# Down projection by Strassen's seven products instead of eight

## The chip, the cores and the metric

The kernel runs on one core of a Trainium2 chip. The metric is the device time of one execution in microseconds (us). TensorE (PE) multiplies, VectorE (DVE), ScalarE (ACT) and GpSimd (POOL) do elementwise work, and SyncE (SP) issues the DMAs. SBUF is the working memory on the chip, PSUM the eight banks into which PE writes.

## The reference

One layer: an attention sub-layer, then the channel sub-layer, with D = 1024 channels, S = 1024 tokens and D_FF = 2816 (22 blocks of 128 rows):

```python
h = rms_norm(x, ln_ffn_pre[l])
f = (jax.nn.silu(h @ w_ffn_gate[l]) * (h @ w_ffn_up[l])) @ w_ffn_down[l]
x = x + rms_norm(f, ln_ffn_post[l])
```

Everything is float32. The change is in the last product, `(...) @ w_ffn_down`, which is [1024 x 2816] times [2816 x 1024].

## The kernel before

Each float32 operand of a product is split into two parts that TensorE takes, high (h) and low (l): `split_sbuf` (L253) has ACT round the operand into h (L254), and POOL or DVE subtract h from the operand to get l (L256). A product of two operands is then three matmuls, h·h, h·l and l·h, into the same PSUM bank (`mm3`, L267 to L269). Nearly all matmuls here are 128x128 weights times 512 columns.

The channel sub-layer has two stages. **Gate and up** (`ffn_gate_up`, L1205) goes over 11 pairs of row blocks of D_FF. For each pair it makes the gate product, then the up product, each by Strassen's seven half-size products (`product`, L1208, matmuls on L1216) over halves of channels, tokens and the pair's two blocks. The sums of the weights are made beside it (`stationary_parts`, L1162, sums on L1180), up to AHEAD = 6 parts ahead of their use. DVE adds the banks into the four results (L1225), ACT applies silu (L1235), DVE or POOL multiplies gate by up (L1240), and the four tiles of 128x512 go to the scratch tensor `s_aa` in HBM (L1242).

**Down** (`ffn_down`, L1271) reads `s_aa` and `w_ffn_down` back in six portions (2, then five times 4 row blocks), 1024 columns of each at a time, splits them, and runs for each of 8 token tiles and 2 column halves all row blocks of the portion into one bank: 22 x 8 x 2 x 3 = 1056 matmuls. ACT copies the bank into the accumulator `X.acc` for the first portion (L1286), DVE adds it for the others (L1288). During the last portion `finish` (L1295) runs after each token tile: ACT squares its two halves (L1308), DVE makes the reciprocal root's argument (L1313, L245), POOL the power (L247), DVE scales both halves (L1319), POOL adds the residual (L1320), and SP writes them out. The last tile does its work on DVE alone (L1310, L1317).

Memory is handed out by allocators in the kernel (`Mem`, `Zone`, `Block`): the large tile AR holds the split parts, AFm the float32 data. The order of the code isn't the order on the chip: the framework orders each engine's instructions itself, by what is ready first, and each engine then runs its own list strictly in order. [rows 12] shows one case.

Of the kernel before, what the change touches and what calls it, by code (L numbers as in the profile page):

```python
# [11 lines left out]
F32 = mybir.dt.float32  # L12
# [6 lines left out]
P = 128  # L19
# [49 lines left out]
AR_COLS = 38912  # L69
AF_COLS = 13568  # L70
# [5 lines left out]
class Mem:  # L76


    def __init__(self, ap, cols):
        self.ap = ap  # L80
        self.busy = np.zeros(cols // GRAN, dtype=bool)
        self.when = np.zeros(cols // GRAN, dtype=np.int64)
        self.clock = 0

# [36 lines left out]
class Block:  # L121
    def __init__(self, mem, lo, cols):
        self.mem, self.lo, self.cols = mem, lo, cols
        self.ap = mem.ap[:, lo:lo + cols]
# [45 lines left out]
def kernel(  # L170
# [47 lines left out]
    s_aa = scratch("s_aa", (NFF * P, S))  # L218
# [5 lines left out]
    AR = big.tile([P, AR_COLS], F32R, name="AR")  # L224
# [68 lines left out]
    mr, mf, mp = Mem(AR, AR_COLS), Mem(AFm, AF_COLS), Psum(PS)  # L293
# [5 lines left out]
    z_ht, z_w, z_q = Zone(mr, (0, 16384)), Zone(mr, (16384, 24576)), Zone(mr, (24576, 32256))  # L299
    z_c, z_ct = Zone(mr, (32768, 34816)), Zone(mr, (34816, AR_COLS))  # L300
    z_kn = Zone(mr, (32256, 32768))
    z_lat, z_qk, z_v = slots(mr, (2, 7)), slots(mr, (7, 9), (12, 14)), slots(mr, (0, 2), (14, 16))
# [5 lines left out]
    z_wc, z_dn = Zone(mr, (28672, AR_COLS)), Zone(mr, (0, AR_COLS))  # L308
    f_ffn, f_acc, f_dn = Zone(mf, (0, AF_COLS)), Zone(mf, (0, 8192)), Zone(mf, (8192, AF_COLS))
# [530 lines left out]
    def mla_proj(M, n, H):  # L840
        wq = load_hl(w_uq[:, n * 192:n * 192 + P].rearrange("(k p) c -> p k c", p=P), f_raw, z_mw, 384, "p (k c) -> p k c", k=3)
        wk = load_hl(w_ukv[:, n * 256:n * 256 + P].rearrange("(k p) c -> p k c", p=P), f_raw, z_mw, 256, "p (k c) -> p k c", k=2)
        qn, kn = z_qk.alloc(SLOT, SLOT), z_qk.alloc(SLOT, SLOT)
# [361 lines left out]
    def ffn_gate_up(X):  # L1205
        banks = Banks(mp, 0, 8)

        def product(bank, i, first):  # L1208
# [9 lines left out]
            w.free()  # L1218

# [8 lines left out]
        for g in range(NFF // 2):  # L1228
            gate = {}
            for u in range(2):  # L1230
                def done(f, c, src):
# [5 lines left out]
                    else:  # L1237
                        s = gate.pop((f, c))
                        e = nc.vector if isinstance(src, Bank) else nc.gpsimd
                        e.tensor_tensor(out=s.ap, in0=s.ap, in1=src.ap, op=ALU.mult)  # L1240
                        r = (2 * g + f) * P
                        nc.sync.dma_start(s_aa[r:r + P, c * 512:(c + 1) * 512], s.ap)  # L1242
                        s.free()
                    src.free()

                a, b, c = banks.alloc(), banks.alloc(), banks.alloc()
                product(a, MB["11"], True)
                s1 = tmp()
                nc.scalar.copy(s1.ap, a.ap)
                product(b, MB["t2"], True)  # L1250
                u2 = add(s1, b)
                product(c, MB["t1"], True)
                product(b, MB["t3"], False)
# [4 lines left out]
                product(a, MB["21"], False)  # L1258
                done(0, 0, a)
                product(b, MB["t4"], False)  # L1260
# [4 lines left out]
                product(c, MB["22"], False)  # L1265
# [3 lines left out]
                done(0, 1, c12)  # L1269

    def ffn_down(X, f0, n):  # L1271
        aa, ws = [], []
        for f in range(f0, f0 + n):
# [164 lines left out]
```

## Time and profile before

| | |
|---|---|
| median of 3 runs | 2034.36 us (2032.48 to 2034.4) |
| profiled execution | 2036.9 us, of which the profile's span is 2035.0 us |
| granted TensorE clock, mean | 0.992 |
| instructions in the span | 29108 |

A time in the rows counts from the span's start. A line of the profile such as `L256 POOL ... AR<-AFm,AR` names the line of the code, the engine, the tile written and the tiles read.

### The profile page before, as it was taken

The numbers are of one execution on the slowest core, as the hardware profiler recorded it, in microseconds if no ns is written. First come the engines' busy times: TensorE is split into PE (matmuls) and PEld (weight loads), VectorE is DVE, ScalarE is ACT, GpSimd is POOL, SyncE is SP. The second block draws the span as 40 slices with busy tenths as digits, with TensorE's granted clock in tenths as the row PEclk, the third lists the DMA queues.
The fourth block names the chain that finished last, engine by engine and source line by source line (L and its number), as shares of the span: only waits on it lengthen the run. The fifth ranks groups of instructions, "written<-read, shape, count | busy, mean of one in ns | idle before, by whom it ended". The sixth has DMA issues, their size and how long they took to land. (4 is left out here: it accounts for less than half of the span.)

```text
span 2035.0 us, 29108 instructions
## 1 busy us (share of the span) xinstructions
PE 1976.3 (97%) x10656; PEld 1715.3 (84%) x10656; DVE 1156.2 (57%) x2464; ACT 864.2 (42%) x1912; POOL 541.0 (27%) x652
## 2 busy tenths in 40 slices
PE   6999999999999999999999998979999999999998
PEld 6898999999898988988978786757888888888886
DVE  7756757676675667786752354575344444353335
ACT  5445444554544446666653333343333333341102
POOL 2000010200000012222121222356564564462214
PEclk9999999999999999999999999989999999999999
DMA  5212111211212031450043533223222222272204
GB/s 169 69 47 81 44 55 53 57 49 42 77 29 80 29 116 50 130 177 29 32 136 103 176 125 103 85 71 94 73 94 84 71 95 73 95 237 83 83 32 145
DMA packets 148494, 176.52 MB, mean 87 GB/s; under 512 B 13536, under 2 KB 117376, under 8 KB 148352
## 3 DMA queue, kind: packets, MB, share of 16 engines
q1 hardware_dynamic: 148352, 174.68, 27.3%
q8 instruction: 83, 1.36, 0.3%
q14 instruction: 59, 0.48, 0.1%
HBM read 130.54 MB, written 44.11 MB: 86 GB/s over the span
## 5 line engine op out<-in xcount | busy, mean ns | idle before, releaser
L267 PE MATMUL PS<-AR 128*128 128x512 f32 (+3 forms) x2216 | 795.1, 361 | 4.0 <-ACT AR L254 2.5
L269 PE MATMUL PS<-AR 128*128 128x512 f32 (+3 forms) x2216 | 786.3, 356 | 2.6 <-POOL AR L256 2.6
L268 PE MATMUL PS<-AR 128*128 128x512 f32 (+3 forms) x2216 | 784.5, 355 | 3.7 <-POOL AR L256 3.7
L254 ACT CAST AR<-AFm 128x512 fp32r<-128x512 f32 (+4 forms) x514 | 301.7, 610 | 514.1 <-PE PS L1216 207.4
L267 PEld LDWEIGHTS PS<-AR 128*128 128x128 f32 x2216 | 418.1, 189 | 56.8 <-ACT AR L260 3.5
L268 PEld LDWEIGHTS PS<-AR 128*128 128x128 f32 x2216 | 419.0, 189 | 47.8 <-POOL AR L256 4.5
L269 PEld LDWEIGHTS PS<-AR 128*128 128x128 f32 x2216 | 417.9, 189 | 46.3 <-POOL AR L256 3.5
L256 POOL TENSOR_TENSOR AR<-AFm,AR 128x512 fp32r<-128x512 f32 (+4 forms) x203 | 309.2, 1529 | 461.7 <-ACT AR L254 397.4
L1216 PE MATMUL PS<-AR 128*128 128x512 f32 x1848 | 425.7, 392 | 6.1 <-POOL AR L256 4.9
L1216 PEld LDWEIGHTS PS<-AR 128*128 128x128 f32 x1848 | 349.3, 189 | 82.2 <-POOL AR L256 6.2
L256 DVE TENSOR_TENSOR AR<-AFm,AR 128x512 fp32r<-128x512 f32 (+5 forms) x311 | 213.1, 714 | 109.3 <-ACT AR L254 81.8
L260 ACT CAST AR<-PS 128x512 fp32r<-128x512 f32 (+3 forms) x320 | 134.5, 440 | 149.5 <-DVE AFm L388 75.4
L1225 DVE TENSOR_TENSOR AFm<-AFm,PS 128x512 f32<-128x512 f32 x110 | 75.2, 684 | 180.3 <-PE PS L1216 179.6
L261 DVE TENSOR_TENSOR AR<-PS,AR 128x512 fp32r<-128x512 f32 (+3 forms) x320 | 152.9, 496 | 38.0 <-ACT AR L260 36.5
L619 POOL CAST AR<-AR 128x128 fp32r<-128x128 f32 (+1 forms) x128 | 43.1, 337 | 456.0 <-PE PS L690 262.4
L649 ACT ACTIVATE AFm<-PS,nm 128x1024 f32<-128x1024 f32 (+3 forms) x192 | 142.5, 745 | 45.9 <-DVE nm L648 28.8
L648 DVE TENSOR_REDUCE nm<-PS 128x1 f32<-128x1024 f32 (+3 forms) x192 | 143.5, 751 | 3.2
L1288 DVE TENSOR_TENSOR AFm<-AFm,PS 128x512 f32<-128x512 f32 x80 | 54.4, 685 | 103.1 <-PE PS L269 103.1
L1180 DVE TENSOR_TENSOR AFm<-AFm 128x512 f32<-128x512 f32 x66 | 70.4, 1066 | 68.4 <-DMA s_aa<-AFm 29.7
L627 POOL MEMSET AR<- 128x256 f32 x64 | 22.3, 349 | 295.3 <-PE PS L269 200.3
L707 PE MATMUL PS<-AR 128*128 128x256 f32 x640 | 94.9, 290 | 0.1
L609 PE MATMUL PS<-idf,AFm 128*128 128x128 f32 x576 | 88.6, 275 | 2.2 <-ACT AFm L741 0.9
(133 smaller groups left out, 1551.9 us busy)
## 6 DMA issues: line engine op xcount, KB each, us to landing
AFm<-in_w_in_dram SPq DMA_DIRECT2D x72, 192.0 KB
AFm<-in_w_ffn_gate_dram SPq DMA_DIRECT2D x22, 512.0 KB
AFm<-in_w_ffn_up_dram SPq DMA_DIRECT2D x22, 512.0 KB
s_aa<-AFm SPq DMA_DIRECT2D x44, 256.0 KB
AFm<-in_w_ffn_down_dram SPq DMA_DIRECT2D x22, 512.0 KB
AFm<-s_aa SPq DMA_DIRECT2D x22, 512.0 KB
AFm<-in_x_dram SPq DMA_DIRECT2D x16, 512.0 KB
AFm<-in_w_in_dram SPq DMA_DIRECT2D x32, 256.0 KB
```

The lines of the kernel that those rows point to most:

```text
L254: nc.scalar.copy(h, src)
L256: e.tensor_tensor(out=l, in0=src, in1=f32v(h), op=ALU.subtract)
L260: nc.scalar.copy(h, src)
L261: nc.vector.tensor_tensor(out=l, in0=src, in1=f32v(h), op=ALU.subtract)
L267: nc.tensor.matmul(o, lhsT=sh, rhs=mh, start=first, stop=False)
L268: nc.tensor.matmul(o, lhsT=sh, rhs=ml, start=False, stop=False)
L269: nc.tensor.matmul(o, lhsT=sl, rhs=mh, start=False, stop=last)
L609: nc.tensor.transpose(tb.ap[:, q * P:(q + 1) * P], C[:, (g + q) * P:(g + q + 1) * P], idf)
L648: nc.vector.tensor_reduce(out=nm[:, m:m + 1], in_=src, axis=ax, op=ALU.max, negate=True)
L649: nc.scalar.activation(out=dst, in_=src, func=ACTF.Exp, bias=nm[:, m:m + 1], scale=1.0, accum_out=ss[:, m:m + 1])
L707: nc.tensor.matmul(sb.ap[:, p * 256:(p + 1) * 256], lhsT=qs.ap[:, m * 256 + v * P:m * 256 + v * P + P], rhs=slots[p]["kT"][:, m, :], start ...
L1216: nc.tensor.matmul(o, lhsT=v[:, ws, k], rhs=m, start=first and k == 0 and x == 0, stop=k == 3 and x == 2, skip_group_check=True)
```

## The change

The down product is done by Strassen's seven products (the form with fifteen additions) too, over halves of tokens (512), of output columns (512) and the two row blocks of a pair. Per pair there are 7 x 4 token tiles x 3 = 84 matmuls, for 11 pairs 924.

- *Token sums in the gate and up stage.* After the up product of a pair, three sums on DVE and one on POOL are made of the four tiles, and seven tiles, not four, go to HBM (`s_a7`).
- *Weight sums.* `down_parts` makes eight differences of 128x512 on DVE for each group of two pairs (the last group has one pair), and splits what the seven products need: 28 parts for a group, 14 of tokens and 14 of weights, every fourth one with its subtraction on DVE, the others on POOL. With one pair there are 14 token parts of 256 columns and 7 weight parts of 512.
- *Products.* Each of the five full groups and the short one runs two token halves (hf), in each the products m1, m6, m5, m7, m2, m4, m3 for two token tiles (tl). m7 and m4 accumulate further into m6's bank, m2 into m1's, m3 into m5's; each product's bank is added to the accumulators by DVE (in the first group copied by ACT, except for m7 and m3). So m7 waits until m6's bank has been read. In the last group POOL adds m1 to three accumulators for each of 4 token tiles, and `finish` runs after m4 and m3; in its second half the order is all products of one token tile, then of the other.
- *Prefetch.* `fill_down` issues further units while four blocks of 1024 columns are free in AR; the first ones during the last seven products of the gate and up stage.
- *Memory.* AR is two tiles now; the second one's place is taken over by the accumulators after the gate and up stage. Two zones of the attention stage (`z_qk`, `z_v`) lie elsewhere.

```diff
+                if u == 1:
+                    x11, x12, x21, x22 = gate[0, 0], gate[1, 0], gate[0, 1], gate[1, 1]
+                    q1 = pair(x21, x22, ALU.add, nc.vector)
+                    q2 = pair(q1, x11, ALU.subtract, nc.vector)
+                    q3 = pair(x11, x21, ALU.subtract, nc.gpsimd)
+                    q4 = pair(x12, q2, ALU.subtract, nc.vector)
+                    for i, t in zip(ORDER, (x11, q2, q1, q3, x12, x22, q4)):
+                        keep(i, t)
...
+    GROUPS = [(g, min(2, NFF // 2 - g)) for g in range(0, NFF // 2, 2)]
+    ORDER = ("m1", "m6", "m5", "m7", "m2", "m4", "m3")
...
+        def part(src):
+            b = z_dn.alloc(1024, 1024)
+            n = src.shape[1]
+            h, l = b.ap[:, 0:n], b.ap[:, n:2 * n]
+            turns[0] += 1
+            split_sbuf(src, h, l, "dve" if turns[0] % 4 == 0 else "pool")
+            return b, h, l
...
+            elif i == "m6":
+                t1 = [diff(v[0, 1], v[0, 0]) for v in B]
+                t2 = [diff(v[1, 1], t.ap) for v, t in zip(B, t1)]
+                ops = [t.ap for t in t2]
...
+    def ffn_down(X):
+        where = {"m1": "a", "m6": "b", "m5": "c", "m7": "b", "m2": "a", "m4": "b", "m3": "c"}
+        for g, kt in GROUPS:
+            first, last = g == 0, g + kt == NFF // 2
+            for hf in range(2):
+                todo = [(i, tl) for i in ORDER for tl in range(2)]
+                if last and hf == 1:
+                    todo = [(i, tl) for tl in range(2) for i in ORDER]
+                for i, tl in todo:
...
+                    for k in range(kt):
+                        _, bh, bl = bs[i][k]
+                        for x, (st_, mv) in enumerate(((sh, bh), (sh, bl), (sl_, bh))):
+                            nc.tensor.matmul(pb.ap, lhsT=st_[:, k, ts_], rhs=mv,
...
+                    for o in to:
+                        if first and i in ("m1", "m6", "m5", "m2", "m4"):
+                            nc.scalar.copy(o, pb.ap)
+                        else:
+                            nc.vector.tensor_tensor(out=o, in0=o, in1=pb.ap, op=ALU.add)
+                    if last and i == "m1":
+                        for o in (acc[t][:, 1], acc[t + 4][:, 1], acc[t + 4][:, 0]):
+                            nc.gpsimd.tensor_tensor(out=o, in0=o, in1=m1, op=ALU.add)
...
+                    if last and i == "m4":
+                        finish(X, t + 4)
+                    if last and i == "m3":
+                        finish(X, t)
...
+    def fill_down():
+        while mr.room(0, AR_CUT) >= 4096:
+            u = next(down, None)
```

## Rows read from the trace of the kernel before

**Rows 1.** The page's first part: busy us, share of the span, instructions.

```profile
PE 1976.3 (97%) x10656; PEld 1715.3 (84%) x10656; DVE 1156.2 (57%) x2464; ACT 864.2 (42%) x1912; POOL 541.0 (27%) x652
```

**Rows 2.** Stretches: busy us (instructions) of PE, PEld, DVE, ACT, POOL; clock, DMA, GB/s.

```profile
1500.00:1600.00 100.00, 99.68 (x440) 82.19 (x439) 40.99 (x55) 31.31 (x52) 55.69 (x41) 1.00 0.27 85
...
1786.00:1900.00 114.00, 114.00 (x504) 94.39 (x503) 50.16 (x49) 35.00 (x44) 40.66 (x17) 1.00 0.42 139
1900.00:2025.00 125.00, 125.00 (x553) 103.49 (x553) 49.55 (x79) 18.14 (x36) 35.55 (x25) 1.00 0.26 89
2025.00:2035.00 10.00, 0.78 (x4) 0.32 (x2) 4.33 (x8) 1.45 (x4) 2.33 (x3) 0.66 0.28 105
```

**Rows 3.** Timeline of PE: the down stage's first and last matmul.

```profile
1786.26 0.39 PE L267 MATMUL PS<-AR 128*128 128x512 f32 x1
...
2025.39 0.39 PE L269 MATMUL PS<-AR 128*128 128x512 f32 x1
```

**Rows 4.** Groups by line: busy us, mean ns, idle us before and what ended it.

```profile
L1216 PE MATMUL PS<-AR 128*128 128x512 f32 x1848 | 425.7, 392 | 6.1 <-POOL AR L256 4.9 <-ACT AFm L1249 0.7 <-DVE AFm L1225 0.3
...
L1288 DVE TENSOR_TENSOR AFm<-AFm,PS 128x512 f32<-128x512 f32 x80 | 54.4, 685 | 103.1 <-PE PS L269 103.1
```

**Rows 5.** Timeline of DVE in the last two finishes: start, us, what.

```profile
2020.38 0.69 DVE L1288 TENSOR_TENSOR AFm<-AFm,PS 128x512 f32<-128x512 f32 x1 [0.81 <-PE PS L269]
2021.92 0.16 DVE L1313 TENSOR_TENSOR ss<-ssh 128x1 f32<-128x1 f32 x1 [0.85 <-ACT AFm L1308]
...
2022.99 1.41 DVE L1319 SCALAR_TENSOR_TENSOR AFm<-AFm,rs_r 128x512 f32<-128x512 f32 x2 [0.73 <-POOL rs_r L247]
...
2027.25 0.67 DVE L1288 TENSOR_TENSOR AFm<-AFm,PS 128x512 f32<-128x512 f32 x1
...
2030.45 1.42 DVE L1317 SCALAR_TENSOR_TENSOR AFm<-AFm,rs_r 128x512 f32<-128x512 f32 x2 [0.73 <-POOL rs_r L247]
```

**Rows 6.** Timeline of POOL in the same finish.

```profile
2022.41 0.55 POOL L247 TENSOR_TENSOR rs_r<-rs_v,mhalf 128x1 f32<-128x1 f32 x1 [1.03 <-DVE rs_v L245]
2023.87 2.91 POOL L1320 TENSOR_TENSOR AFm<-AFm 128x512 f32<-128x512 f32 x2 [0.92 <-issue]
```

**Rows 7.** Timeline of ACT in the same finish.

```profile
2021.16 0.63 ACT L1308 ACTIVATE AFm<-AFm 128x512 f32<-128x512 f32 x1 [0.70 <-DVE AFm L1288]
```

**Rows 8.** Timeline of DVE inside the gate and up stage.

```profile
1590.77 2.64 DVE L1180 TENSOR_TENSOR AFm<-AFm 128x512 f32<-128x512 f32 x2 [0.98 <-issue]
...
1607.55 0.69 DVE L256 TENSOR_TENSOR AR<-AFm,AR 128x512 fp32r<-128x512 f32 x1
1608.15 0.68 DVE L1225 TENSOR_TENSOR AFm<-AFm,PS 128x512 f32<-128x512 f32 x1
```

**Rows 9.** Timeline of POOL at the same place.

```profile
1589.87 1.29 POOL L1240 TENSOR_TENSOR AFm<-AFm 128x512 f32<-128x512 f32 x1 [2.87 <-DVE AFm L1225]
1591.14 1.72 POOL L256 TENSOR_TENSOR AR<-AFm,AR 128x512 fp32r<-128x512 f32 x1
```

**Rows 10.** Single lines: duration in ns, min/median/max.

```profile
L1288 DVE TENSOR_TENSOR AFm<-AFm,PS x80: 673/686/689, 1819.9 to 2027.3; 128x512 f32<-128x512 f32 x80
...
L1180 DVE TENSOR_TENSOR AFm<-AFm x63: 681/842/1753, 1356.2 to 1753.0; 128x512 f32<-128x512 f32 x63
...
L256 POOL TENSOR_TENSOR AR<-AFm,AR x18: 2388/2410/3399, 1790.0 to 1942.2; 128x1024 fp32r<-128x1024 f32 x18
```

**Rows 11.** Groups by line and shape, from 1300 us on.

```profile
L254 ACT CAST AR<-AFm 128x512 fp32r<-128x512 f32 x173 | 106.5, 621 | 253.1 <-PE PS L1216 207.4 <-issue 29.1 <-DMA AFm<-in_w_ffn_up_dram 3.7
...
L1180 DVE TENSOR_TENSOR AFm<-AFm 128x512 f32<-128x512 f32 x64 | 69.0, 1078 | 56.0 <-DMA s_aa<-AFm 29.7 <-DMA AFm<-in_w_ffn_up_dram 11.5 <-issue 8.6
```

**Rows 12.** Timeline of ACT at the end of the gate and up stage.

```profile
1765.33 1.05 ACT L254 CAST AR<-AFm 128x1024 fp32r<-128x1024 f32 x1 [2.75 <-DMA AFm<-s_aa]
...
1770.14 0.59 ACT L1249 COPY AFm<-PS 128x512 f32<-128x512 f32 x1 [1.36 <-PE PS L1216]
```

**Rows 13.** Who waited for whom in SP's queue, gate and up stage.

```profile
SPq L1168 <- POOL AR L256: 167.8, 37, 8.1
```

More of the change, by code (lines that the diff above doesn't have):

```diff
@@ L69 @@
 AR_COLS = 38912
+AR_CUT = 30720
 AF_COLS = 13568
@@ L76, with __init__ @@
 class Mem:
-    def __init__(self, ap, cols):
-        self.ap = ap
+    def __init__(self, *aps):
+        self.aps, cols = [], 0
+        for ap in aps:
+            self.aps.append((cols, ap))
+            cols += ap.shape[1]
         self.busy = np.zeros(cols // GRAN, dtype=bool)
@@ L83, in __init__, with view, room @@
         self.clock = 0
+    def view(self, lo, cols):
+        at, ap = [x for x in self.aps if x[0] <= lo][-1]
+        assert lo + cols - at <= ap.shape[1]
+        return ap[:, lo - at:lo - at + cols]
+    def room(self, lo, hi):
+        return GRAN * int((~self.busy[lo // GRAN:hi // GRAN]).sum())
     def release(self, lo, cols):
@@ L1206, in ffn_gate_up, with product @@
         banks = Banks(mp, 0, 8)
-        def product(bank, i, first):
+        def product(bank, i, first, end):
             X.fill()
@@ L1218, in product @@
             w.free()
+            if end:
+                for q in range(4):
+                    mr.release(7168 * q + 1024 * i, 1024)
+                X.fill_down()
         def tmp():
@@ L1230, in ffn_gate_up @@
             for u in range(2):
+                end = u == 1 and g == NFF // 2 - 1
                 def done(f, c, src):
@@ L1257, in ffn_gate_up @@
                 done(1, 1, c22)
-                product(a, MB["21"], False)
+                product(a, MB["21"], False, end)
                 done(0, 0, a)
-                product(b, MB["t4"], False)
+                product(b, MB["t4"], False, end)
                 c21 = add(s1, b)
@@ L1264, in ffn_gate_up @@
                 done(1, 0, c21)
-                product(c, MB["22"], False)
+                product(c, MB["22"], False, end)
                 c12 = add(u2, c)
@@ L1269, in ffn_gate_up @@
                 done(0, 1, c12)
[L1271 to L1293 removed]
+                if u == 1:
[6 more added lines that the diff above has]
+                        keep(i, t)
+                        t.free()
+                    x21.free()
@@ L1395, in fill @@
             X.parts.append(b)
-    X.fill = fill
+    X.down, down, X.wl = [], down_parts(), None
+    def fill_down():
+        while mr.room(0, AR_CUT) >= 4096:
+            u = next(down, None)
+            if u is None:
+                return
+            X.down.append(u)
+    X.fill, X.fill_down = fill, fill_down
     mix_out(X, prefetch)
-    h2 = mr.ap[:, 0:28672]
-    X.h2v = h2.rearrange("p (q i h c) -> p q i h c", q=4, i=7, h=2)
+    X.h2v = AR[:, 0:28672].rearrange("p (q i h c) -> p q i h c", q=4, i=7, h=2)
     ffn_gate_up(X)
-    for b in X.h2:
-        b.free()
-    X.dn = Banks(mp, 0, 8)
+    X.m1 = [f_m1.alloc(512, 512) for _ in range(4)]
+    AFb = turn.tile([P, AR_COLS - AR_CUT], F32, tag="turn", name="AFb")
+    f_acc = Zone(Mem(AFb), (0, 8192))
     X.acc = [f_acc.alloc(D, 1024) for _ in range(NT)]
-    down = [ffn_down(X, 0, 2)] + [ffn_down(X, f0, 4) for f0 in range(2, NFF, 4)]
-    next(down[0])
-    for i, d in enumerate(down):
-        if i + 1 < len(down):
-            next(down[i + 1])
-        next(d, None)
+    ffn_down(X)
 _INS = ['x', 'positions', 'ln_mix_pre', 'w_in', 'lambda_q1', 'lambda_k1', 'lambda_q2', 'lambda_k2', 'da_subln',
```

151 lines of the change are left out of this document (112 added, 39 removed).

## The prediction

> **What bounds the kernel now.** I read the engines' shares first: PE is busy 97% of the span, DVE 57%, ACT 42%, POOL 27% [rows 1]. A busy share of PE is not yet a bound, so the stages come next: in the gate and up stage and through the down stage PE has no gap at full clock (100 of 100 us, 114 of 114, 125 of 125), while DVE and POOL have room, POOL 56 of 100 us in the first and 41 of 114 in the second [rows 2]. The idle times agree: PE lost 6.1 us in all before the 1848 gate and up matmuls, and in the down stage it is DVE that waited for PE, 103.1 us [rows 4]. So the down stage costs what its matmuls cost. From its first matmul to its last plus one step (1786.26 to 2025.6) there are 1056 in 239.3 us, 0.2267 us each [rows 3]. From there to the end of the span lie 9.4 us of the last tile's norm.
>
> **The matmuls.** 1056 become 924 of the same shape: 132 x 0.2267 = **29.9 us** less, as long as PE stays without gaps. A full group then takes 168 x 0.2267 = 38.1 us, the five of them 190.4 us, the last group 19.0 us. The rest of the sum is what the other engines make of that.
>
> **What DVE and POOL share.** An instruction of DVE with two operands in SBUF and one of POOL don't run at the same time here. POOL's product from 1589.87 ends at 1591.16; the first of two DVE sums, issued at 1590.77, falls in it; POOL's next takes 1.72 in place of 1.29, and DVE's second sum ends 0.55 after that, so two sums of 0.6 took 2.64 [rows 8, 9]. One DVE instruction thus held POOL up by 0.43 us. Sums on SBUF run from 681 to 1753 ns, while evictions, with one operand in PSUM, stay within 673 to 689 [rows 10].
> The Trainium skill (SBUF — State Buffer, Who interferes with whom) has the same as a lock: a DVE instruction with two SBUF inputs contends with a POOL instruction that reads SBUF, and the loser "fully blocks"; with one SBUF input it doesn't. By that rule the forecast below stands; if the two merely overlapped, the sum would be the 2021 of the first rival. The rows here bear the rule out.
>
> **A full group of the down stage** (38.1 us of PE):
> - POOL: 21 of 28 subtractions x 1.29 [rows 9] = 27.1 us. DVE: 7 subtractions and 8 differences, each 0.60 from start to start [rows 8] = 9.0 us, holding POOL up 15 x 0.43 = 6.5. POOL with that: 33.6 us of 38.1.
> - DVE besides: 28 evictions x 0.69 [rows 10] = 19.3 us, so 28.3 without waits. ACT: 28 x 0.62 [rows 11] = 17.4 us.
> - DVE's waits for POOL: at worst each of the 15 waits out a whole POOL instruction, 19.4 us, DVE 47.7, and the group is 9.6 us longer than PE's 38.1: +48 us for five. At best, none of it reaches PE: 0 (less than nothing is excluded, as matmuls without gaps can't be closer). The nearest row: the sums of the gate and up stage took 1.08 on the mean against 0.68 alone, a wait of 0.40 [rows 10, 11] with POOL busy 0.56 [rows 2]; at POOL's 0.71 that is 0.5, DVE 36 us of 38.1.
> At 95%, in strict order, DVE isn't a bound but a queue. What stands in it behind a sum that waits is evictions, and PE waits for those: m7 can't start in m6's bank until it is read, and between m6's end and m7's start for a tile lie 3 x 6 matmuls = 4.1 us. Four differences in a row, each alternating with a POOL instruction, take 4 x 1.7 = 6.8. So I expect PE to lose something in each group and take a quarter of the way to the worst case: **+12 us** (0 to 48).
>
> **The last group** is where most is given back. Before, the part of the span that answers to it is 84 matmuls plus the 9.4 us: 28.4 us, for the finishes were spread over 44 us of matmuls, one each 5.44 us. Now all eight finishes, 28 evictions and 12 extra POOL sums stand against 19.0 us of matmuls.
> - POOL: 12 + 14 sums x 1.29 = 33.5, eight powers x 0.55 [rows 6] = 4.4, held up by 16 DVE instructions x 0.43 = 6.9: 44.8 us. It starts 1.8 us in (m1's 3 matmuls, its eviction), and after the last power come 4.6 us, from the last scaling at 2030.45 to the end of the span [rows 5]. Floor: 51.2 us.
> - Ceiling, if DVE keeps each finish whole before it takes the next eviction: from an eviction's end (2021.07) to the end of the scaling (2024.40) 3.33 us [rows 5], by a square more (0.73, [rows 7] and its read-out) after m4, where both halves wait: 4 x 4.75 + 3 x 4.02 with their evictions, 7.75 for the last (2027.25 to the end), 20 other evictions = 13.8, the start 0.9, and some 10.5 in which evictions of m6 wait for POOL's sums (four ahead of m6's second tile, a finish's two sums and one more in each pass of the second half): 64 us.
> The order isn't that of the code: the framework put a cast of the down stage ahead of a copy of the stage before it [rows 12]. So I go nearer the floor's side, without reaching it, since the list is fixed beforehand: 57 us, **+28.6** against 28.4 (22.8 to 35.6). If PE falls to its lower clock in the gaps (0.66 in the last row of [rows 2], after it stopped), the m7 and m4 that evictions wait for add up to 5.4 us (24 matmuls x 0.227) within that ceiling.
>
> **Gate and up.** Per pair DVE gets three sums, POOL one, some 11 x (3 x 0.60 + 1.29) = 34 us in all if it all fell on PE. It is covered: DVE is busy 41 of 100 us there and POOL 56 [rows 2], weight parts are six products ahead (6 x 2.72 us), and the next eviction that PE needs has a whole product of 2.72 us. Seven writes and not four per pair add 33 x 256 KB, 21 GB/s beside 85; SP's queue, where the next weight load stands behind the writes, already waits 167.8 us for POOL to free buffers, at most 8.1 at a time [rows 13], inside the 16 us of lead. 0, up to 34. In the down stage 31.7 MB in some 200 us are 158 GB/s, where 139 took 0.42 of the DMA engines [rows 2]: 0. Memory moves and the accumulators' new place, free once the last gate and up matmul has run: 0, as the first eviction into it comes two products later; a few us either way in the attention stage, where I see no wait that they add.
>
> **The sum.** 2035.0 − 29.9 + 12 + 28.6 = 2045.7 of span; the profiled execution lies 1.9 above its span, and 2.5 above the median of the runs, so **2045 us**.
>
> **Rivals.**
> 1. *Faster: the queues never reach PE.* DVE's waits stay under the 4.1 us of slack in every group, and the last group packs down to its floor: 2035 − 29.9 + 22.8 = 2028, 2027 as a median; without any exclusion between DVE and POOL 6.9 less, some 2021. It decides on whether m6's evictions come within 4.1 us. For it: POOL and DVE each have 5 to 12% spare in a group, and units are prepared 9 or more ahead. Were the last group's work hidden altogether, 2005; its POOL work alone (38 us) speaks against that.
> 2. *No change:* 2 us lost in the groups and 28.6 in the last one: 2035.
> 3. *Slower by more: DVE's queue is the bound.* 24 to 48 us in the groups: 2057 to 2081. For it: bursts of four differences; against: the mean wait of 0.40.
> 4. *Slower, in the gate and up stage:* the sums hold up evictions there, by up to 34: up to 2079. Against: the cover above.
> That the change doesn't cut the matmuls to 924 can't be, by its loops.
>
> **Chances.** My forecast, 2039 to 2057, 0.40; rival 1, 0.26; rival 2, 0.16; rival 3, 0.13; rival 4, 0.05. A measurement tells 0.2% (4 us) from no change. Faster 0.26, the same 0.16, slower 0.58. The range runs from 2020, the first rival's packed case, to 2070, inside the third.
>
> **What would show it.** Right: in the trace after, 924 matmuls on the down stage's line, gaps of PE of a few hundred ns to some us ended by DVE evictions in each full group, longest after m6; from the last group's first matmul to the end 51 to 64 us with POOL busy throughout and PE mostly idle. Wrong: full groups without gaps (then the 12 is nothing), a last group much under 51 us (then POOL's sums overlap more than I think), or PE waiting in the gate and up stage by more than its 6 us of now.

## The result, and the profile after

The changed kernel takes **2116.18 us** (median of 4, 2114.78 to 2122.17) beside 2034.38 us for the kernel before (4 runs): a ratio of **1.0413**, interval 1.0396 to 1.0430. The forecast was slower, 2045, and the range ended at 2070, so both the amount and the range were wrong. (The ratio is an estimate of its own and not the quotient of the two medians, 1.0402, which lies in the interval.) The profiled execution's span is 2113.8 us, 78.8 more than before.

The first row answers to [rows 1], the second fence to [rows 2] (columns as there).

```profile
PE 1985.2 (94%) x10524; PEld 1700.1 (80%) x10524; DVE 1315.3 (62%) x2627; ACT 905.0 (43%) x2033; POOL 700.7 (33%) x774
```

```profile
1500.00:1600.00 100.00, 94.17 (x404) 75.19 (x403) 51.63 (x60) 31.65 (x55) 56.75 (x39) 1.00 0.26 85
...
1936.30:1940.00 3.70, 0.40 (x2) 0.03 (x1) 3.70 (x6) 0.62 (x1) 3.48 (x3) 0.89 0.42 135
1940.00:1945.00 5.00, 5.00 (x12) 3.94 (x13) 3.54 (x6) 0.00 (x0) 0.00 (x0) 0.50 0.28 95
1945.00:1980.00 35.00, 35.00 (x154) 28.93 (x153) 25.20 (x32) 15.39 (x27) 27.14 (x19) 0.99 0.41 136
...
2055.50:2113.80 58.30, 24.94 (x86) 16.99 (x84) 41.45 (x63) 10.48 (x32) 41.30 (x34) 0.70 0.27 99
```

PE is busy only 9 us more, with 132 matmuls fewer; DVE has 159 us more and POOL 160. In the gate and up stage, where PE had 100 of 100 us, it now has 94 (first window), though no other engine but its weight loads is busy for more than 57 of 100. Next the timeline of PE (start, us, operation, count, and in brackets the idle time before it and what ended it); it answers to [rows 3].

```profile
1505.94 8.66 PE L1230 MATMUL PS<-AR,ARb 128*128 128x512 f32 x36 [1.97 <-DVE AFm L1243]
...
1541.64 3.06 PE L1230 MATMUL PS<-AR,ARb 128*128 128x512 f32 x12 [1.97 <-DVE AFm L1243]
...
1824.91 5.86 PE L1230 MATMUL PS<-AR,ARb 128*128 128x512 f32 x24 [3.51 <-DVE AFm L1243]
1830.61 8.34 PE L1417 MATMUL PS<-AR 128*128 128x512 f32 x36
1843.61 7.34 PE L1417 MATMUL PS<-AR 128*128 128x512 f32 x24 [4.66 <-ACT AFb L1425]
1857.01 34.63 PE L1417 MATMUL PS<-AR 128*128 128x512 f32 x144 [6.06 <-DVE AFb L1427]
1895.41 41.28 PE L1417 MATMUL PS<-AR 128*128 128x512 f32 x168 [3.78 <-DVE AFb L1427]
1940.00 41.15 PE L1417 MATMUL PS<-AR 128*128 128x512 f32 x168 [3.31 <-DVE AFb L1427]
1984.45 76.08 PE L1417 MATMUL PS<-AR 128*128 128x512 f32 x321 [3.30 <-DVE AFb L1427]
```

L1230 is the gate and up matmul, L1417 the down matmul, L1243 and L1427 the evictions by DVE. From such rows each span divides at the first matmul of either stage and the first of the last group (the 841st of the down line, its start counted back from the end of its block at 0.2267 us each):

| us | before | after | difference | forecast |
|---|---|---|---|---|
| start of gate and up | 1347.7 | 1350.3 | +2.7 | 0 |
| gate and up | 438.6 | 480.3 | **+41.7** | **0** |
| five full groups (190.4 of matmuls) | | 225.0 | **+34.6** | **+12** |
| last group | 28.4 | 58.2 | +29.8 | +28.6 |
| 132 matmuls fewer | | | −29.9 | −29.9 |
| sum | | | +78.9 | +10.7 |

The stage that I had priced at nothing cost most. The +2.7 at the start says nothing: in the runs below, none of which changes the attention stage's instructions, the gate and up stage starts between 1345.5 and 1350.1. The groups by line (from 1300 us on; columns as in [rows 4]) show who waited:

```profile
L1230 PE MATMUL PS<-AR,ARb 128*128 128x512 f32 x1464 | 354.5, 401 | 27.8 <-DVE AFm L1243 21.4 <-POOL ARb L270 2.4 <-ACT ARb L268 1.6
...
L1417 PE MATMUL PS<-AR 128*128 128x512 f32 x924 | 228.7, 410 | 41.2 <-DVE AFb L1427 25.0 <-DVE rs_v L259 7.1 <-ACT AFb L1425 4.7
...
L1326 DVE TENSOR_TENSOR AFm<-AFm 128x512 f32<-128x512 f32 x44 | 53.6, 1231 | 20.9 <-POOL AR L270 13.9 <-DMA AFm<-in_w_ffn_down_dram 7.0
...
L1268 DVE TENSOR_TENSOR AFm<-AFm 128x512 f32<-128x512 f32 x33 | 38.6, 1171 | 26.4 <-POOL AFm L1260 25.7
```

PE waits for DVE's evictions in both stages. The two kinds of sums that the change adds, L1268 (token sums) and L1326 (weight differences), take 1171 and 1231 ns where one alone takes 681 [rows 10]. What this does to PE is seen in DVE's own timeline, here at one gap of each stage:

```profile
1533.40 0.69 DVE L1268 TENSOR_TENSOR AFm<-AFm 128x512 f32<-128x512 f32 x1 [1.41 <-POOL AFm L1260]
1534.01 1.78 DVE L1194 TENSOR_TENSOR AFm<-AFm 128x512 f32<-128x512 f32 x1
1535.72 0.68 DVE L1268 TENSOR_TENSOR AFm<-AFm 128x512 f32<-128x512 f32 x1
1536.32 0.68 DVE L1194 TENSOR_TENSOR AFm<-AFm 128x512 f32<-128x512 f32 x1
1536.92 1.78 DVE L1268 TENSOR_TENSOR AFm<-AFm 128x512 f32<-128x512 f32 x1
1538.62 0.68 DVE L270 TENSOR_TENSOR ARb<-AFm,ARb 128x512 fp32r<-128x512 f32 x1
1539.23 1.76 DVE L1194 TENSOR_TENSOR AFm<-AFm 128x512 f32<-128x512 f32 x1
1540.91 0.68 DVE L1243 TENSOR_TENSOR AFm<-AFm,PS 128x512 f32<-128x512 f32 x1
...
1932.40 2.88 DVE L1326 TENSOR_TENSOR AFm<-AFm 128x512 f32<-128x512 f32 x2
1935.20 0.68 DVE L1427 TENSOR_TENSOR AFb<-AFb,PS 128x512 f32<-128x512 f32 x1
1935.80 1.18 DVE L270 TENSOR_TENSOR AR<-AFm,AR 128x512 fp32r<-128x512 f32 x1
1936.90 0.68 DVE L1427 TENSOR_TENSOR AFm<-AFm,PS 128x512 f32<-128x512 f32 x1
1937.50 1.16 DVE L1326 TENSOR_TENSOR AFm<-AFm 128x512 f32<-128x512 f32 x1
1938.58 0.67 DVE L1427 TENSOR_TENSOR AFm<-AFm,PS 128x512 f32<-128x512 f32 x1
1939.18 1.27 DVE L1427 TENSOR_TENSOR AFb<-AFb,PS 128x512 f32<-128x512 f32 x2
```

From 1533.40 to 1540.91 DVE works without a pause on seven instructions with two operands in SBUF, and only then on the eviction that the matmuls of 1541.64 wait for. At 1541.64 PE has been idle for 1.97 us. The engine is half empty over 100 us and full over the 8 us that count. In the down stage sums and evictions alternate, and the two-operand instructions (L1326 and L270 here) take 1.16 us and more where one alone takes 0.68; the first eviction of the row at 1939.18 is the one that the matmuls of 1940.00 wait for.

The Trainium skill (SBUF — State Buffer, Who interferes with whom) names what sets the two kinds apart: a DVE instruction with at most one SBUF input, outside DVE's two-port modes, doesn't contend with GpSimd. The trace agrees: all 110 evictions L1243 took 673 to 690 ns, the sums among them up to 1.78 us.

### The profile page after: what moved, and what is told of

It is laid out like the page before. It is cut to its first block, busy times and chain, and to the rows that moved or that the text cites. A ratio compares the mean times of both kernels' runs of the same rounds, so it can differ in the third digit from the quotient of the medians.

```text
span 2113.8 us, 29579 instructions
## 1 busy us (share of the span) xinstructions
PE 1985.2 (94%) x10524; PEld 1700.1 (80%) x10524; DVE 1315.3 (62%) x2627; ACT 905.0 (43%) x2033; POOL 700.7 (33%) x774
## 3 DMA queue, kind: packets, MB, share of 16 engines
q1 hardware_dynamic: 170992, 191.98, 28.6%
## 5 line engine op out<-in xcount | busy, mean ns | idle before, releaser
L281 PE MATMUL PS<-AR 128*128 128x512 f32 (+3 forms) x1368 | 501.6, 368 | 3.5 <-ACT AR L268 2.9
L283 PE MATMUL PS<-AR 128*128 128x512 f32 (+3 forms) x1368 | 494.8, 362 | 2.1 <-POOL AR L270 2.1
L282 PE MATMUL PS<-AR 128*128 128x512 f32 (+3 forms) x1368 | 492.3, 360 | 3.8 <-POOL AR L270 3.8
L270 POOL TENSOR_TENSOR AR<-AFm,AR 128x512 fp32r<-128x512 f32 (+3 forms) x206 | 300.4, 1479 | 273.0 <-ACT AR L268 228.9
L1230 PE MATMUL PS<-AR,ARb 128*128 128x512 f32 x1464 | 354.5, 401 | 27.8 <-DVE AFm L1243 21.4
L268 ACT CAST AR<-AFm 128x512 fp32r<-128x512 f32 (+5 forms) x461 | 248.2, 574 | 290.0 <-PE PS L1417 98.6
L1230 PEld LDWEIGHTS PS<-AR,ARb 128*128 128x128 f32 x1464 | 277.6, 191 | 102.0 <-DVE AFm L1243 27.1
L281 PEld LDWEIGHTS PS<-AR 128*128 128x128 f32 x1368 | 258.5, 189 | 30.0 <-ACT AR L268 3.4
L282 PEld LDWEIGHTS PS<-AR 128*128 128x128 f32 x1368 | 259.0, 189 | 27.4 <-POOL AR L270 4.2
L283 PEld LDWEIGHTS PS<-AR 128*128 128x128 f32 x1368 | 258.3, 189 | 26.3 <-POOL AR L270 3.0
L1417 PE MATMUL PS<-AR 128*128 128x512 f32 x924 | 228.7, 410 | 41.2 <-DVE AFb L1427 25.0
L1417 PEld LDWEIGHTS PS<-AR 128*128 128x128 f32 x924 | 182.9, 200 | 86.8 <-DVE AFb L1427 22.9
L270 DVE TENSOR_TENSOR AR<-AFm,AR 128x512 fp32r<-128x512 f32 (+4 forms) x255 | 169.5, 698 | 77.3 <-ACT AR L268 50.0
L270 POOL TENSOR_TENSOR ARb<-AFm,ARb 128x512 fp32r<-128x512 f32 (+2 forms) x96 | 133.9, 1406 | 136.4 <-ACT ARb L268 131.9
L1243 DVE TENSOR_TENSOR AFm<-AFm,PS 128x512 f32<-128x512 f32 x110 | 75.0, 683 | 150.4 <-PE PS L1230 148.5
L281 PE MATMUL PS<-ARb,AR 128*128 128x256 f32 (+2 forms) x470 | 153.3, 328 | 1.1 <-DVE ARb L275 0.5
L282 PE MATMUL PS<-ARb,AR 128*128 128x256 f32 (+2 forms) x470 | 151.0, 321 | 0.0
L283 PE MATMUL PS<-ARb,AR 128*128 128x256 f32 (+2 forms) x470 | 150.2, 320 | 0.0
```

Of the source, the lines that this page charges most:

```text
L268: nc.scalar.copy(h, src)
L270: e.tensor_tensor(out=l, in0=src, in1=f32v(h), op=ALU.subtract)
L281: nc.tensor.matmul(o, lhsT=sh, rhs=mh, start=first, stop=False)
L282: nc.tensor.matmul(o, lhsT=sh, rhs=ml, start=False, stop=False)
L283: nc.tensor.matmul(o, lhsT=sl, rhs=mh, start=False, stop=last)
L1230: nc.tensor.matmul(o, lhsT=v[:, ws, k], rhs=m, start=first and k == 0 and x == 0, stop=k == 3 and x == 2, skip_group_check=True)
```

## The experiments

Theory A throughout: instructions of DVE and POOL with both operands in SBUF stand in each other's way, and evictions stand behind them in DVE's list. The rivals differ by place. Stage times come from profiled executions; that of the gate and up stage differs by some 9 us between kernels that leave it unchanged (480.3, 481.6, 486.9 and 489.4 in the four that change the down stage alone), so smaller differences there say nothing. The five groups of runs that leave the groups alone differ too (215.0 to 225.7), more by what the lower clock costs after the gaps (4.9 to 13.5 us) than by the gaps (18.4 to 23.3 us).

### The address of the second part of AR

In the trace, matmuls with weights in ARb took 394 ns (median), those in AR 389, and from start to start 0.2333 us against 0.2267. With 1464 of them that is 9.8 us of PE's time. The first run moves ARb by 32 bytes, from byte 196128 to 196160; the second puts it behind AR at byte 140416.

```diff
-    ARb = turn.tile([P, AR_COLS - AR_CUT], F32R, tag="turn", name="ARb")
+    ARb = turn.tile([P, AR_COLS - AR_CUT + 8], F32R, tag="turn", name="ARb")[:, 8:]
...
```

> The changed kernel with its second part of AR (and the accumulators that take its place) moved by 32 bytes, so that it begins on a multiple of 64 bytes in a partition; nothing else. In the trace after, the gate and up matmuls whose weights lie in the second part take 394 ns (median) where those with weights in the first take 389, and one follows the other in 0.233 us in place of 0.227. Theory A, the address: all go back to 389 ns, the stage of 480 us (1350.3 to 1830.6) is 8 to 10 us shorter, span about 2105. Rival, the split into two tiles as such (waits on two tiles): 394 stays, no change, 2114.

Measured: 2112.30 us, ratio 1.0397 (1.0382 to 1.0413); matmuls 392 ns, the stage 482.0. Alignment is a part of it at most.

```diff
-    AFm = big.tile([P, AF_COLS], F32, name="AFm")
+    rest = ctx.enter_context(tc.tile_pool(name="rest", bufs=1))
+    AFm = rest.tile([P, AF_COLS], F32, name="AFm")
...
```

> The changed kernel with the second part of AR right behind the first in SBUF (at byte 140416 of a partition; it lay at 196128, or 196160 in the run that only aligned it), where the same weights lay before the change, and the float32 tile behind it. Matmuls with weights there took 394 ns, 392 when aligned to 64 bytes, 389 before the change. Theory, the address: 389 ns, the gate and up stage 7 to 10 us shorter than 480, span about 2105. Rival, the two tiles (each matmul waits on and signals for both): 392 to 394 stays, no change.

Measured: 2109.60 us, ratio 1.0377 (1.0361 to 1.0392); 389 ns, but the stage still 480.8. The matmuls got faster, and PE waited longer (30.6 us of gaps from 1384 us on, 26.6 before the edit): with the sums in place, the side engines set the pace. The whole span is 4.1 us shorter (2109.7), but that lies ahead of the stage, which starts at 1345.8 here. Whether the 9.8 us count without the sums is asked of the run with all additions left out, below, which changes other things too.

### The token sums, and what about them costs

```diff
-                    q1 = pair(x21, x22, ALU.add, nc.vector)
...
-                    for i, t in zip(ORDER, (x11, q2, q1, q3, x12, x22, q4)):
+                    for i, t in zip(ORDER, (x11, x12, x21, x22, x12, x22, x11)):
...
```

> The changed kernel without the three DVE sums and the POOL sum of a pair; seven tiles are still written, some of them twice the same, so the result of the down product is left out of account. The stage of gate and up is 41.6 us longer after the change (480.3 against 438.6), 27.8 us of it in gaps of PE that mostly end with an eviction on DVE. Theory A, the sums on DVE (the first waits for POOL's product, each may wait out a POOL instruction, and evictions stand behind them): the gaps fall to about the 6 us of before, the stage to about 455 (the address effect of some 9 us stays, and the end of the stage, where the down parts begin, some 5), span about 2089. Rival B, the seven writes, which hold up the weight loads in SP's queue: stage stays within 5 us of 480.

Measured: 2085.22 us, ratio 1.0259 (1.0244 to 1.0275), the stage 452.1. The four sums of each pair, with the buffers that they hold, cost 28 us. The three additional writes don't:

```diff
-                    for i, t in zip(ORDER, (x11, q2, q1, q3, x12, x22, q4)):
+                    for i, t in zip(ORDER, (x11, q2, q1, q3)):
...
```

> The changed kernel with all four sums made, but only four of the seven tiles written (the others read back in their place, so the down product's input is partly replaced). Theory A, the sums on DVE: the gate and up stage stays within 5 us of 480. Rival B, the writes in SP's queue: the stage falls by 20 to 30 us, as the loads of weights come earlier. The two together, should both be needed: 5 to 15 us.

Measured: 2112.96 us, ratio 1.0399 (1.0381 to 1.0416), the stage 483.2.

If DVE's list is the trouble, should the sums go to POOL?

```diff
-                    q1 = pair(x21, x22, ALU.add, nc.vector)
+                    q1 = pair(x21, x22, ALU.add, nc.gpsimd)
...
```

> The changed kernel with all four token sums of a pair on POOL. Theory A (without the sums the gate and up stage took 452 us in place of 480, so DVE's sums and what stands behind them cost some 28 us): DVE no longer waits for POOL's product, POOL gets 3 x 1.29 = 3.9 us more for each pair of 38, its instructions hold up DVE's weight sums a little more; the stage falls to 452 to 462 us, span 2088 to 2098. Rival, the exclusion alone counts, whoever makes the sums: the stage stays over 470.

Measured: 2143.44 us, ratio 1.0547 (1.0531 to 1.0562), the stage 513.6: A's number missed, and on the wrong side; the rival's "over 470" holds, but it doesn't say why the stage gets 33 us longer. The timelines of POOL and of DVE at one pair's end show why:

```profile
1540.61 6.39 POOL L1268 TENSOR_TENSOR AFm<-AFm 128x512 f32<-128x512 f32 x4
1546.96 2.49 POOL L1194 TENSOR_TENSOR AFm<-AFm 128x512 f32<-128x512 f32 x2
```

```profile
1548.25 1.74 DVE L1194 TENSOR_TENSOR AFm<-AFm 128x512 f32<-128x512 f32 x1 [3.77 <-POOL AFm L1194]
1549.92 0.67 DVE L1243 TENSOR_TENSOR AFm<-AFm,PS 128x512 f32<-128x512 f32 x1
```

The four sums stand ahead of POOL's weight sums, DVE waits 3.77 us for the first of these, and the eviction stands behind. So it isn't one engine's time but both lists, and what crosses between them.

Three runs ask whether it is the work of the sums or the buffers that they hold (four of 512 columns in the zone from which the raw weights, 2048 columns each, are loaded too).

```diff
-                    q1 = pair(x21, x22, ALU.add, nc.vector)
...
+                    for q, z in ((q1, x21), (q2, x11), (q3, x22), (q4, x12)):
+                        nc.scalar.copy(q.ap, z.ap)
```

> Leaves out the four token sums of each pair: four ACT copies of the tiles fill the same buffers, and the same seven writes follow. Theory A (the sums' own time on DVE and POOL, and the lock between them, hold up the evictions): the gate and up stage 450 to 460 us, as without sums (452), median 2084 to 2092. Rival (what costs is that the four extra buffers and the eviction of gate into them come later, or ACT's queue): the stage stays at 475 to 483, median 2107 to 2113.

Measured: 2103.28 us, ratio 1.0348 (1.0329 to 1.0368), the stage 473.9: A missed, and the time lies next to the rival's. Without any sum on DVE or POOL, 22 of the 28 us remain.

```diff
...
+                    for q, z in zip(qs, (x21, x11, x22, x12)):
+                        nc.scalar.copy(q.ap[:, 0:8], z.ap[:, 0:8])
...
+                        nc.sync.dma_start(s_a7[g, n + 3][:, 0:8], t.ap[:, 0:8])
...
```

> Leaves out the four token sums of each pair; four buffers of 512 columns are taken at the same place all the same, ACT copies 8 columns into each (four short instructions), three tiles are written whole and the four buffers' 8 columns, and then they are given back. Theory A (memory: the raw weights' buffers of the next pairs come free later, the weight sums that need them bunch up on DVE, and evictions queue behind): the gate and up stage 468 to 480 us, median 2100 to 2112, as with the full copies (473.6). Rival (the work: what ACT's full copies cost was ACT's time): 450 to 457, as without sums (452), median 2082 to 2090.

Measured: 2095.26 us, ratio 1.0319 (1.0303 to 1.0334), the stage 469.9: the buffers alone, with next to no work, keep 18 of the 28 us of the stage. The median is only 10 us above that of the run without sums, below A's forecast, for the five groups took 215.0 here and 225.1 there: after three of its five gaps the clock stayed full. The opposite, the work without the buffers:

```diff
-    z_wc, z_dn = Zone(mr, (28672, AR_CUT), (AR_CUT, AR_COLS)), Zone(mr, (0, AR_CUT))
+    z_wc, z_qs, z_dn = Zone(mr, (AR_CUT, AR_COLS)), Zone(mr, (28672, AR_CUT)), Zone(mr, (0, AR_CUT))
...
-                    t = tmp()
+                    t = z_qs.try_alloc(512) or tmp()
```

> The four token sums are written to 2048 columns of AR (taken from the zone of the split weight parts, which keeps 8192 columns for 8 parts in place of 10) and not to the zone of the raw weights. They come out rounded to the matmul's type, so the result is less exact. Theory A (memory): the stage 455 to 468 us where it is 480, median 2090 to 2104. Rival (the work of the sums on DVE and POOL): 478 to 490, median 2112 to 2124; so too if the two parts fewer now hold up the splits.

Measured: 2097.73 us, ratio 1.0327 (1.0310 to 1.0345), the stage 474.8, between the two forecasts, the median inside A's. All weights lie in ARb here, the 384 others too, which is 2.6 us of it at 0.0067 each.

What the buffers do is seen in SP's queue (who waited for whom: us, times, longest; gate and up stage), from the kernel after, the one without sums, the one that holds buffers, and the one with room, in this order; it answers to [rows 13]:

```profile
SPq L1182 <- POOL ARb L270: 170.1, 15, 15.3
```

```profile
SPq L1182 <- POOL ARb L270: 138.3, 23, 8.2
```

```profile
SPq L1182 <- POOL ARb L270: 198.2, 15, 16.0
```

```profile
SPq L1182 <- POOL ARb L270: 156.2, 38, 8.0
```

The load of a raw weight waits for buffers that POOL's subtractions free. Before, no wait was above 8.1 us; with four more buffers in use the longest is 15.3, with the buffers alone 16.0, and with room elsewhere 8.0 again. Late loads reach DVE, whose weight sums (L1194, 1400 to 1780 us, same four kernels) wait for the DMA. In the run that holds buffers two of them start at 1576.18 after 7.22 us of such waiting, right ahead of the eviction that ends a gap of 2.84 us on PE:

```profile
L1194 DVE TENSOR_TENSOR AFm<-AFm 128x512 f32<-128x512 f32 x54 | 65.5, 1219 | 33.2 <-DMA AFm<-in_w_ffn_up_dram 24.0 <-DMA AFm<-in_w_ffn_gate_dram 7.6 <-issue 0.9
```

```profile
L1194 DVE TENSOR_TENSOR AFm<-AFm 128x512 f32<-128x512 f32 x55 | 61.2, 1113 | 18.7 <-DMA AFm<-in_w_ffn_gate_dram 5.8 <-issue 5.8 <-DMA AFm<-in_w_ffn_up_dram 5.0
```

```profile
L1194 DVE TENSOR_TENSOR AFm<-AFm 128x512 f32<-128x512 f32 x54 | 69.6, 1299 | 37.2 <-DMA AFm<-in_w_ffn_up_dram 24.0 <-DMA AFm<-in_w_ffn_gate_dram 6.1 <-DMA s_a<-AFm 5.5
```

```profile
L1194 DVE TENSOR_TENSOR AFm<-AFm 128x512 f32<-128x512 f32 x55 | 69.4, 1261 | 27.3 <-issue 8.4 <-DMA AFm<-in_w_ffn_gate_dram 7.8 <-POOL AFm L1260 6.3
```

The 24.0 us of waiting for the up weights come with the buffers and go with them. But with the loads in time PE still has one gap of 1.44 us in each pair, ended by an eviction: the work on its own costs nearly as much. Either is enough for most of the 28 us, and the two aren't additive. How much of the last run is due to the two split parts fewer that it leaves room for stays open; PE waited 3.7 us for an ACT cast there, once, at the stage's start.

Last, the same sums at another place:

```diff
...
                 product(c, MB["t1"], True, end)
+                if u == 0 and held:
+                    sums(*held.pop(0))
...
```

> The four token sums of a pair are issued later, between the third and fourth product of the next pair's gate (the last pair's at once); nothing is left out. Theory A (the 29 us that the sums cost come from their meeting POOL's product, its weight sum and the weight subtractions at the end of a pair): the stage 455 to 470 us where it is 480, median 2090 to 2104. Rival (DVE and POOL are full enough that they cost the same wherever they stand): 478 to 490, median 2112 to 2124.

Measured: 2094.82 us, ratio 1.0310 (1.0293 to 1.0327), the stage 467.3, with gaps near 0.9 us where they were near 2. Away from the end of the pair 13 of the 28 us come back. Nothing is left out here.

### The full groups of the down stage

POOL's 21 subtractions of each group are replaced by ACT copies, two in place of a cast and a subtraction, so the subtraction is left out:

```diff
-            split_sbuf(src, h, l, "dve" if turns[0] % 4 == 0 else "pool")
+            if turns[0] % 4 == 0:
+                split_sbuf(src, h, l, "dve")
+            else:
+                nc.scalar.copy(h, src)
+                nc.scalar.copy(l, src)
```

> The changed kernel with POOL taken out of the splitting in the down stage: where POOL subtracts, ACT copies instead (the low part is replaced by a copy of the operand, which leaves the subtraction out). DVE's instructions are the same. The five full groups take 224.9 us after the change, 34.5 more than their matmuls at 0.2267 us, with one gap of PE of 3.3 to 3.8 us per group before m7 and a low clock behind it. Theory A, DVE's two-operand instructions wait out POOL's, so that evictions come late: the gaps vanish, five groups in 190 to 197 us, span some 30 us shorter. Rival B, DVE's own load and order (28.3 us per group, four differences in a row): the gaps stay, over 215 us. ACT has 30 of 38 us then; if it becomes late, PE waits for ACT and not for DVE.

```profile
1826.21 195.36 PE L1421 MATMUL PS<-AR 128*128 128x512 f32 x861
```

The differences on DVE in this run (minimum, median, maximum in ns), where L1326 had a mean of 1231 before the edit:

```profile
L1330 DVE TENSOR_TENSOR AFm<-AFm x36: 680/687/694, 1833.5 to 1981.1; 128x512 f32<-128x512 f32 x36
```

Measured: 2079.00 us, ratio 1.0228 (1.0210 to 1.0246). PE's timeline shows 861 matmuls without a gap, the five groups take 190.4. DVE's own load isn't the cause; that POOL works beside it is. All 36 differences in the stretch of the five groups now take 680 to 694 ns. The other half of the pair, DVE's eight differences of a group left out:

```diff
-                t1 = [diff(v[0, 1], v[0, 0]) for v in B]
-                t2 = [diff(v[1, 1], t.ap) for v, t in zip(B, t1)]
-                ops = [t.ap for t in t2]
+                ops = [v[1, 1] for v in B]
...
```

> The changed kernel without the eight weight differences of a group on DVE (the products take unsummed weights, so the differences are left out). POOL's splitting stays. Theory A, DVE instructions with two operands in SBUF wait out POOL's and evictions stand behind them: 7 of 15 such instructions are left in a group, never several in a row, so PE runs without gaps after the first group, five groups in 190 to 200 us in place of 224.9, span some 2080 to 2090. Rival, POOL is too slow by itself (27.1 us of 38.1 with the lock's 3): gaps stay, ended by POOL.

```profile
1844.90 7.19 PE L1413 MATMUL PS<-AR 128*128 128x512 f32 x24 [7.20 <-ACT AFb L1421]
1853.61 181.85 PE L1413 MATMUL PS<-AR 128*128 128x512 f32 x801 [1.51 <-DVE AFb L1423]
```

Measured: 2091.00 us, ratio 1.0287 (1.0271 to 1.0302). Four groups run without a gap; only the first loses 10.8 us (201.2 in all, just above A's 200), 7.20 of it to ACT's copies of the first banks. So of the 34.6 us some 24 come from differences that meet POOL's subtractions.

The first group's wait for ACT goes back to POOL too. In the kernel after:

```profile
1830.47 8.55 POOL L270 TENSOR_TENSOR AR<-AFm,AR 128x512 fp32r<-128x512 f32 x6
1838.97 1.26 POOL L1260 TENSOR_TENSOR AFm<-AFm 128x512 f32<-128x512 f32 x1
1840.27 0.58 ACT L1425 COPY AFm<-PS 128x512 f32<-128x512 f32 x1 [6.56 <-POOL AFm L1260]
```

ACT's first copy goes to m1's buffers in AFm, and the profile names POOL's product of gate and up (L1260) as what released it; that product stands behind six subtractions for the down stage. In the run without POOL's subtractions the first group has no gap at all.

### The last group

```diff
-                    if last and i == "m1":
-                        for o in (acc[t][:, 1], acc[t + 4][:, 1], acc[t + 4][:, 0]):
-                            nc.gpsimd.tensor_tensor(out=o, in0=o, in1=m1, op=ALU.add)
```

> The changed kernel without the twelve POOL sums of m1 in the last group (left out of the result). The last group takes 58.3 us from its first matmul to the end of the span. My reckoning, POOL's work as its floor: 15.5 us of POOL less and no evictions that wait for those sums; 40 to 46 us, span 12 to 18 shorter, some 2098. Rival, the chain of eight finishes on DVE sets the time (38.9 us of evictions, squares, power and scaling in a row, with other evictions 64): 53 us or more, span at most 5 shorter.

Measured: 2106.10 us, ratio 1.0363 (1.0346 to 1.0381), the last group 49.6: 8.6 us less, between the two forecasts. Twelve sums of 1.29 are 15.5 us of POOL's work; some half of it was on the path, and the rest wasn't.

```diff
-                    if last and i == "m1":
+                    if g == GROUPS[-2][0] and i == "m3":
                         for o in (acc[t][:, 1], acc[t + 4][:, 1], acc[t + 4][:, 0]):
...
+                            if last and i == "m1":
+                                nc.tensor.matmul(bank[tl, "b"].ap, lhsT=st_[:, k, ts_], rhs=mv, start=k == 0 and x == 0,
...
```

> The twelve POOL sums of m1 stand in the second-last group instead of the last one (after m3 of its second half's first token tiles); in the last group m1's three matmuls are repeated into m6's bank, 12 matmuls more (2.7 us), and m1 has no eviction there. Theory A (the last group is as long as POOL's and DVE's queues; leaving the sums out took 8.5 us off it): the last group 48 to 51 us where it was 58.3, the groups before it unchanged, median 2107 to 2111. Rival (POOL's work costs as much wherever it stands, since DVE waits for it there too): the second-last group takes 5 to 10 us more, median 2114 to 2118.

Measured: 2106.48 us, ratio 1.0365 (1.0342 to 1.0389); the last group 49.3, the five others 219.4. Moving the sums gives as much as leaving them out, and the 12 more matmuls cost nothing where PE waits anyway.

### The sum of it

```diff
...
+                    for i, t in zip(ORDER, (x11, x12, x21, x22, x12, x22, x11)):
...
+                ops = [v[1, 1] for v in B]
...
+                    if g == GROUPS[-2][0] and i == "m3":
...
```

> Leaves out all the additions of operands of the seven products (the four token sums: tiles are written instead; the eight weight differences: halves are used unsummed), has AR's second part right behind its first, and m1's POOL sums in the second-last group; matmuls, splits, evictions and finishes are all there. It bounds what the idea could give if those additions were free. Theory (the losses add up: sums 28, differences 24, the last group 8 us): 2116 - 60 = 2056, 2046 to 2062, so not faster than the kernel before (2032 to 2034) even then. Rival (with the additions gone PE runs without gaps in the five groups and the stage, and only the last group's finishes are left): 2034 - 30 + 20 = 2024, up to 2035.

Measured: 2032.29 us (10 runs) against 2032.39 (13): ratio **1.0003**, 0.9994 to 1.0013. The theory's number missed: it is 24 us faster than adding up the losses gave, and no faster than before. It lies inside the rival's "up to 2035", 8 us above its 2024. The losses sum to more together than one by one: with sums, differences and address all gone the gate and up stage has no gap after 1384 us and takes 437.2 (438.6 before), 14.9 less than without the sums alone. That fits the 9.8 us of the address (its matmuls follow one another by 0.2267 us here), which no run gives back alone without the sums, and the two gaps (1.07 and 3.48) that were left near the stage's end, where the first differences of the down stage are made. What is left is 200.5 for the groups (10.1 above the matmuls, all in the first one) and 48.9 for the last:

```profile
1783.12 8.32 PE L1414 MATMUL PS<-AR 128*128 128x512 f32 x36
1798.99 184.99 PE L1414 MATMUL PS<-AR 128*128 128x512 f32 x805 [7.55 <-ACT AFb L1425]
```

10.1 + 20.5 for the last group (48.9 against 28.4) eat up the 29.9 us that the matmuls gave. So in this arrangement the form only breaks even when its operand additions are free. That is not its limit: nothing shows that the first group must lose 10.1 us, and without POOL's subtractions it lost none.

The version with everything that helped, nothing left out (late sums, ARb placed, m1's sums moved):

> Nothing left out: the sums made later (gave 19 to 21 us), m1's POOL sums out of the last group (gave 8 to 10), and AR's second part right behind its first (gave 2 to 5). By the sum 2114 - 20 - 9 - 3 = 2082, 2078 to 2088; with the faster matmuls of the stage now free of gaps up to 7 us less, 2075. Rival (the gains stand in each other's place, as the address did alone): 2090 to 2096. Neither comes near the 2032 of before.

Measured: 2079.27 us, ratio 1.0237 (1.0222 to 1.0252), as forecast; stage 458.7, groups 223.0, last 49.4. It beats the change by 37 us and stays 48 behind the kernel before.

## Why the prediction was wrong, point by point

- **Matmuls, −29.9: right.** 924 on the down line, 0.2267 us apart; without gaps the five groups took the forecast 190.4.
- **Last group, +28.6: the number was right, in part by luck** (58.2 us against 57, inside 51 to 64). POOL's queue was to be the floor, with "POOL busy throughout"; POOL was busy 41 of the 58 us, as was DVE, and leaving out 15.5 us of POOL's sums gave 8.6. The rest of the path isn't POOL's, and no run takes it apart.
- **Full groups, +12: the mechanism was right, the size was not** (+34.6, inside the 0 to 48). Groups 2 to 4 have one gap each (3.3 to 3.8 us), before m7 of the first token half, ended by m6's eviction, as worked out. The first has two (4.66 and 6.06). The fifth has none: while it runs only the short group's parts are made, and POOL is busy 19.4 of 38.1 us, where it was 31.3 of 44.4 in the third. The run without POOL's subtractions takes all gaps away, the one without differences those after the first group. Two things were mis-sized. The mean wait was not one of them (0.5 for each of 15 assumed; 0.55 for the differences, 1231 less 681 ns; 0.34 for DVE's subtractions, 1016 less 681): a quarter of the way to the worst case, 2.4 us a group, had no row behind it. The working's own burst, 6.8 us against 4.1 of slack, with the 0.69 of the eviction itself, gives 3.4, and the trace has 3.3 to 3.8. And I counted gaps only: of the 34.6, PE's idle time is 21.1 (the view by line of that stretch); the other 13.5 us are matmuls after a gap. After the 3.31 us gap that ends at 1940.00, the clock is 0.50, the lower of its two levels, for 5 us, 12 matmuls where 22 go at full clock, and full (0.99) after that. I had allowed for that in the last group and not here. The first group adds a wait that I hadn't seen, 4.66 us for ACT's copies, which wait for POOL's last products. I had put the accumulators' new place at 0 by looking at the matmuls alone.
- **Gate and up, 0: wrong, and the step that failed.** It cost 41.7. The cover that I named was an average ("DVE is busy 41 of 100 us there and POOL 56") and a lead of six parts. Three things were missed. (1) The averages hid the place: the sums fall together at the end of a pair with POOL's product and the weight sums, and at 1541.64 the eviction of t2 stands behind 7.5 us of it. PE is done with t2 at some 1536.9 (counted back from the gap by one product) and DVE starts the eviction at 1540.91, 4.0 us later. Between t2 and t3, which needs the bank, lies one product, t1, of 2.8 us. "The next eviction that PE needs has a whole product" was so, but a whole product was too little. (2) The sums hold four buffers in the zone that feeds the weights. I priced the writes and the queue, not the memory; the longest wait of a weight load went from 8.1 to 15.3 us, about the whole lead of 16, and the held buffers alone bring 18 of the 28 us. (3) "Memory moves: 0": ARb's place makes its matmuls 0.0067 us slower each, 9.8 us of PE's time, but giving them back changed nothing as long as the sums hold PE up (480.8). Of the 41.7 as PE's time, gaps after 1384 us are 26.6 and the slower matmuls 9.8; the rest, 5.3, is the lower clock behind gaps and the stage's start, which no run separates.
- **The chances.** Rival 3 (24 to 48 in the groups) and rival 4 (up to 34 in gate and up) came true together, the second beyond its bound: 34.6 + 41.7. I gave them 0.13 and 0.05 as cases apart. They share a mechanism, two-operand work of DVE and POOL ahead of evictions (in gate and up beside the held buffers), and if it holds in one stage it is likelier in the other; the range ended at 2070 because no case had both.

## What to carry to other kernels

When work is added to an engine that is half idle, look at the few microseconds where it lands and at what is queued behind it there, not at the busy share; and ask which buffers it holds, and what is loaded into them next. A saving in matmuls is worth its time only if the additions it is paid with run on engines with room beside each other: run the version in which they are left out first, since here it showed that this arrangement had nothing to win.

## What was not expected of the hardware

- Weights in the tile at byte 196128 made a matmul of 512 columns last 394 ns (median) and follow the last by 0.2333 us; at 196160 392 ns, at 140416 389 ns and 0.2267. The rows (minimum, median, maximum, from the kernel after and the placed one):

```profile
L1230 PE MATMUL PS<-AR,ARb x1464: 388/394/796, 1354.4 to 1830.4; 128*128 128x512 f32 x183
```

```profile
L1231 PE MATMUL PS<-AR,ARb x1464: 387/389/797, 1349.4 to 1826.3; 128*128 128x512 f32 x183
```

  Whether the address's alignment or its height counts, these three places don't tell.
- A gap of 3.3 us can cost PE about as much again in clock, or nothing: 3.31 us before 1940.00, and then 41.15 us for 168 matmuls that take 38.2 without it; but in the run without m1's sums, after a gap of the same length at the same place, the granted clock stayed 1.00 (1942.52 to 1980):

```profile
1942.52 38.36 PE L1417 MATMUL PS<-AR 128*128 128x512 f32 x168 [3.30 <-DVE AFb L1427]
```

  The runs with m1's sums moved and with buffers held show the same once each (38.33 us after 3.30). What decides it, these runs don't tell.
